# Where the operands of TensorE's products begin within a 64-byte line

## The chip, the cores and the metric

The kernel runs on one core of a Trainium2 chip. The metric is the device time of one execution in microseconds (us). Each comparison is between runs on the same chip.

## What is computed

One layer of a hybrid mixer over 1024 latent tokens and 256 context tokens, with a model width of 1024. The heads of both branches are 8, of width 128.

```python
h  = rms_norm(x) * (1 + scale) + shift            # the same for the context, with its own modulation
cols = h @ w_in                                    # q, k, v, z of branch A; q, k, v, z of branch B; two gates
# branch A: short convolution and silu on q, k, v; chunked gated delta rule in both directions
s_next = s * exp(gl) + kd.T @ (u - w @ s)
o_a    = qd @ s + qk @ v_new
# branch B: differential attention, two softmaxes a head, latents read context and latents
attn = softmax(q0 @ k0.T) - lam * softmax(q1 @ k1.T)
o_b  = attn @ v
# both branches: norm, silu gate, projection; then the merge
merged = g_a * (y_a @ w_oa) + g_b * (y_b @ w_ob)
out    = x + gate * (merged @ w_out)
```

All of it is float32. The large products are done in three parts with rounded operands (float32r): every factor is split into a high part, which is the rounded value, and a low part, the rest, and high x high, high x low and low x high are added up in PSUM.

## The kernel before

Everything is tiled to 128 partitions. A product on TensorE has a loaded operand (128 columns of weights, one weight load for each product) and a moving operand (256, 288 or 512 columns that stream past it). In the code `mm(out, lhsT, rhs)` at L55 loads `lhsT` and moves `rhs`; nearly all products go through its line L56, and turns (transposes on TensorE) through L63.

The stages in order of time:
- `front` (to about 105 us): loads, the normed tokens `hs` in high and low parts (`hgroup`), the modulation, and the first projection.
- `conv_start`, `conv_weights`, `conv_flow` (to about 400 us): projections of branch A's q, k, v. There the weights `wh`, `wl` are loaded and the tokens `hs` move, 512 or 256 columns at a time. Two parts of the kind "t" (the first two pairs of branch B's values) turn this round: `hs` is loaded and `wh`, `wl` move, 288 columns (with the columns for the decay gates) or 256.
- `part_weights`, `part_flow` (about 390 to 745 us): branch B's keys, further values and queries, ten parts, all in the turned-round form: `hs` loaded, 256 columns of `wh`, `wl` moving. Branch A's scan preparation (`gdn_prep`: `gram`, substitution on VectorE) runs between.
- `weights`, `fill_flow` (to about 1300 us): 32 units for the gates, 512 columns of `hs` moving, beside branch A's scan in float32 (`chain`, `out`).
- attention (about 1300 to 1755 us): `scores` (tile `s`: `qh`, `ql` loaded, `kk` moving), softmax on ScalarE, VectorE and GpSimd, `turns` (tile `t`: `S` loaded, the identity in `ct` moving), `high` and `low` (the turned weights in parts `ah`, `al`, L1636 and L1641), `att_out` (tile `v`: `vh`, `vl` loaded, 256 columns of `ah`, `al` moving), and branch A's merge `merge_` (tile `ma`, `y` moving).
- `b_main` (about 1766 to 1853 us): branch B's merge (tile `mb`): `wh`, `wl` of the pool `ws2` loaded, 512 columns of `yh`, `yl` of the pool `yq` moving.
- `o_main` (to the end): the output projection by seven half-size products (tiles `x`, `z`): `ah`, `al` loaded, `bh`, `bl` moving, from the pool `lp` for the even ones, `rp` and `bp` for the odd ones.

The order of every engine's instructions is written out by a planner inside the kernel: generators yield steps with an estimated cost, and `flow` or `turn_flow` picks the next one. It plans with costs alone, and not with addresses.

Addresses come from pools that lie in two stacks in each partition, one growing from the left, one from the right. A pool rounds each tile up to 32 bytes. A pool's tiles with the same tag share a place. Float32 words have 4 bytes, so 8 words are 32 bytes and 16 words one line of 64 bytes. In the kernel before, all operands of rounded products begin at a multiple of 64 bytes.

Of the kernel before, what the change touches and what calls it, by code (L numbers as in the profile page):

```python
# [8 lines left out]
F32 = mybir.dt.float32  # L9
F32R = mybir.dt.float32r  # L10
# [7 lines left out]
P = 128  # L18
D = 1024
KT = D // P  # L20
L = 1024
LC = 256
LT = L + LC
# [6 lines left out]
W = 256  # L30
# [13 lines left out]
class Block:  # L44
# [150 lines left out]
    def setup(self):  # L195
        nc, a = self.nc, self.a
        cp = self.cp = self.pool("const")
        self.dp = self.pool("spill", space=DRAM)
        ct = cp.tile([P, 3, P], F32, name="ct")
        nc.sync.dma_start(ct, a["consts"].rearrange("(a p) n -> p a n", p=P))  # L200
        self.ident, self.up, self.lo = (ct[:, i, :] for i in range(3))
        self.one = self.lo[:, 0:1]
        self.mhalf = cp.tile([P, 1], F32, name="mhalf")
        nc.gpsimd.memset(self.mhalf, -0.5)
        self.da = self.dp.tile([H, 2 * NT, 4, 32, 32], F32, name="da")
        self.db = self.dp.tile([H, 2 * NT, 4, 32, 32], F32, name="db")
        self.ya = self.dp.tile([2, H, P, L], F32, name="ya")
        self.yb = self.dp.tile([H, P, L], F32, name="yb")
        self.gkq = self.dp.tile([H, P, LT + L], F32, name="gkq")
        self.gkk = self.dp.tile([H, LT, P], F32, name="gkk")  # L210
        self.gv = self.dp.tile([H, LT, P], F32, name="gv")
        self.sza = self.dp.tile([H, P, L], F32, name="sza")
        self.szb = self.dp.tile([H, P, L], F32, name="szb")
        self.qd = self.dp.tile([2, H, P, L], F32, name="qd")
        self.kd = self.dp.tile([2, H, P, LT], F32, name="kd")
        self.vd = self.dp.tile([2, LT, H * P], F32, name="vd")
        self.gt = self.dp.tile([2 * KT, P, L], F32, name="gt")
        self.ma = self.dp.tile([KT, P, L], F32, name="ma")
        self.xq = self.dp.tile([H, P, 2, NT // 2, 2, 2, P], F32, name="xq")
        self.tbd = self.dp.tile([2, P, 1024], F32, name="tbd")  # L220
        self.gcd = self.dp.tile([2, H, LT], F32, name="gcd")
        self.gad = self.dp.tile([1, D], F32, name="gad")
        self.rbd = self.dp.tile([H, L], F32, name="rbd")
        for n in ("gkq", "gkk", "gv", "sza", "szb", "qd", "kd", "vd", "gt", "gcd", "ya", "yb"):
            self.dbg[n] = getattr(self, n).name


    @staticmethod
    def later(t, us):

        return t[0], t[1] + us

    def bank(self, name):

# [3 lines left out]
    def front(self, st, early, kv0):  # L238

        nc, a, cp, V = self.nc, self.a, self.cp, self.nc.vector  # L240
# [67 lines left out]
        def weights():  # L308
            for i, n in ((0, W), (1, W + 32)):
                yield lambda: (f"w{i}", 1) in T  # L310
                hl, ends = [self.wab[1 - i].tile([P, KT, n], F32R, tag=t, name=t) for t in ("wh", "wl")], []
                for s in range(2):
                    k = slice(s * KT // 2, (s + 1) * KT // 2)
                    for o, rw, us in ((0, raws[s], 0.256), (W, grw[:, k], 0.032))[:1 + i]:
                        c = slice(o, o + rw.shape[2])
                        t1 = yield ACT, 0.1 + 3.6 * us, [T[f"w{i}", s], T.get(("mm", 3))], lambda: nc.scalar.copy(hl[0][:, k, c], rw)
                        t2 = yield DV2, 4.7 * us, [t1], lambda: V.tensor_tensor(
                            hl[1][:, k, c], rw, hl[0][:, k, c].bitcast(F32), ALU.subtract)
                        ends += [t1, t2]
                    self.raw_t[s] = t2  # L320
                    if i == 0:
                        T["w", s] = [t1, t2]
                T["hl"] = T.get("hl", hl)
                if i:
                    self.parts_[1] = *hl, ends
# [122 lines left out]
    def conv_start(self, cols, right, late):  # L448

        self.copyq, self.tapq, self.siluq, self.normq, self.evq = [], [], [], ([], []), []  # L450
        self.copied, self.out_t, self.cdone, self.sq_t = {}, {}, set(), [None, None]
        self.row_t, self.sides, self.ringed = None, 0, 0
        self.ctiles = sum(2 for kind, _ in cols if kind in range(3))
        pools, last = self.wab, len(cols) - 1
        for q, b in ((self.copyq, 0), (self.tapq, 1), (self.siluq, 2), (self.normq[0], 2.5), (self.normq[1], 2.5), (self.evq, 0)):
            self.stream(self.forever(q), b)
        for g, b in ((self.gates(), 0.5), (self.lam_setup(), 0.6), (self.qk_tables(), 4), (self.gate_row(), 4)):
            self.stream(self.side(g), b)
        self.stream(self.conv_weights([c for _, c in cols], pools), 3)
        self.stream(self.conv_flow(cols), 9)  # L460
        done = lambda: len(self.cdone) >= self.ctiles and self.sides == 4 and not self.ringed
        self.stream(self.first(done, right, late), 6)
        self.turn_flow(lambda: last in self.parts_ and self.parts_done == last and self.head and not self.evq)
        self.ahead = self.parts_.pop(last)
        self.wab = pools if last % 2 else pools[::-1]
        self.streams = []
# [18 lines left out]
            x = next(g) if callable(x) else g.send((yield x))  # L485
        self.head = g, x

    def conv_weights(self, cols, pools):
        raw = lambda s: (self.wr.tile([P, KT // 2, W], F32, tag="wr", name="wr"), self.raw_t[s])
        for i, c0 in enumerate(cols):  # L490
            if i > 1:
                yield lambda: self.parts_done >= i - 1
                yield from self.weight(raw, *(pools[(i + 1) % 2].tile([P, KT, W], F32R, tag=n, name=n) for n in ("wh", "wl")),
                                       c0, W, [self.part_t.get(i - 2)], self.parts_, i, (DV2, DV2))

    def conv_flow(self, cols):
# [401 lines left out]
    def part_weights(self, parts):  # L898
        raw = lambda s: (self.wr.tile([P, KT // 2, W], F32, tag="wr", name="wr"), self.raw_t[s])
        for i, p in enumerate(parts):  # L900
            if i:
                yield lambda: self.parts_done >= i - 1
                yield from self.weight(raw, *(self.wab[i % 2].tile([P, KT, W], F32R, tag=n, name=n) for n in ("wh", "wl")),
                                       self.part_cols(*p), W, [self.part_t.get(i - 2)], self.parts_, i, (POOL, DV2))

    def fill_flow(self, todo):
# [178 lines left out]
    def gdn_prep(self, h):  # L1085
# [6 lines left out]

        def keys():
            S = lambda nm, shape: self.gh[0].tile(shape, F32, tag=nm, name=nm)
            kq, qk = S("kq", [P, LT + L + 8])[:, :LT + L], S("qk", [P, 2, 2, 2, P])
            kT, qT = kq[:, :LT], kq[:, LT:]
            tk = yield DMA, 3.3, self.kT_t, lambda: nc.sync.dma_start(kq, self.gkq[h])
            tk = tq = self.later(tk, 1.5)
            return kT, qT, qk, tk, tq
# [5 lines left out]
        for d in range(2):  # L1105
            for c in range(NT):
                t = yield ACT, 0.293, [self.later(ld, 2.0)], lambda: nc.scalar.activation(
                    X[:, d, c], X[:, d, c], AF.Abs, bias=self.gcc[:, c, d * H + h:d * H + h + 1], scale=-1.0)
            te[d] = yield ACT, 1.18, [t], lambda: nc.scalar.activation(X[:, d], X[:, d], AF.Exp, scale=-1.0), AF.Exp
        yield lambda: self.gram == h  # L1110
        kT, qT, qk, tk, tq = mine or (yield from keys())

        tX, tQ = [[], []], []
        for c0 in range(0, NT, 2):
            yield self.psum()
            b = self.banks.pop(0)
            pt = PT("gram")
            for j in range(2):
                c = c0 + j
                kc = kT[:, c * P:(c + 1) * P]  # L1120
                t = yield PE, 0.2235, [tk, b], lambda: self.mm(pt[:, j * 256:j * 256 + P], kc, kc)
                if c < NL:
                    t = yield PE, 0.2235, [tk, tq, b], lambda: self.mm(pt[:, j * 256 + P:j * 256 + 256], kc, qT[:, c * P:(c + 1) * P])
# [503 lines left out]
    def high(self, y, b, k, pt, t, bank):  # L1627

        nb, q = min(4, NT - 4 * k), slice(b * P, b * P + P)
        if b == 0:  # L1630
            yield lambda: self.open_ and self.vdone[k] >= y["i"]
            for a in ("ah", "al"):
                y[a, k] = self.a1.tile([P, nb, W], F32R, tag=f"{a}{k}", name=a)
            y["old", k], y["in", k] = self.vfree[k], []
        pv = pt[:, :nb * P].rearrange("p (j f) -> p j f", f=P)
        e = yield ACT, 0.48 if nb == 4 else 0.27, [t, y["old", k]], lambda: self.nc.scalar.copy(y["ah", k][:, :, q], pv)  # L1636
        self.lows.append((2 * y["i"] + 1, self.low(y, k, pv, q, e, bank)))
# [198 lines left out]
    def closing(self, zr, st, side):  # L1836
# [6 lines left out]
        self.a0s.close()  # L1843
        self.bp = self.spool(zr, "bp", side="right")
        for n in "hl":
            self.bp.tile([P, 4, 512], F32R, tag=f"b{n}", name="b" + n)
        sy = zr.enter_context(ExitStack())
        self.yq, self.stage = self.spool(sy, "yq", side="right"), 1
        yield lambda: H - 1 in self.yk and not self.groups and not self.mouts and self.wdone >= 16
# [361 lines left out]
```

## Time and profile before

| | |
|---|---|
| median of 3 runs | 1937.08 us (1934.67 to 1939.23) |
| profiled execution | 1935.46 us |
| its span, first to last instruction | 1933.3 us |
| mean granted clock of TensorE | 1.000 |
| busy: PE, PEld, DVE, ACT, POOL | 1896.7, 1675.3, 1453.0, 1062.6, 678.8 us |

PE is TensorE's products, PEld its weight loads, which overlap them, DVE is VectorE, ACT ScalarE, POOL GpSimd, SP the engine that issues the DMAs. A row of a group gives line, engine, operation, what is written <- what is read (moving operand first), shapes, count, then busy us and mean ns of one, then the idle time before them and what ended it. The mean of a product is its time in flight; the next one begins inside it.

### The profile page before, as it was taken

The page shows a single profiled execution, that of the slowest core. Times are in us where ns is not written, and L with a number is a line of the kernel's source. Part 1 is how long each engine was busy: PE and PEld are TensorE (multiplying, and loading weights), DVE is VectorE, ACT ScalarE, POOL GpSimd, SP SyncE. Part 2 cuts the span into 40 slices and gives each one's busy share as a digit, 9 for nine tenths or more (in the row PEclk, how much of TensorE's full clock was granted, in tenths as well). Part 3 has the DMA queues.
Part 4 walks back from the last instruction along what each step waited for, and adds up shares of the span by engine and source line. Part 5 has one row for each costly group of instructions (what it writes and reads, how often), then busy time and mean ns, then how long its engine had stood idle before and what let it go on. Part 6 is the DMA issues. An engine that isn't in the chain of part 4 may idle for free.

```text
span 1933.3 us, 37454 instructions
## 1 busy us (share of the span) xinstructions
PE 1896.7 (98%) x13807; PEld 1675.3 (87%) x13807; DVE 1453.0 (75%) x3613; ACT 1062.6 (55%) x2189; POOL 678.8 (35%) x610
## 2 busy tenths in 40 slices
PE   6999999999999999999999999999999999999999
PEld 4878888899999998888888888888997888888887
DVE  4687998957887887867865865338996979995677
ACT  4543444426233563677576645439885868884222
POOL 3200000005441342343333332336766667672203
PEclk9999999999999999999999999999999999999999
DMA  9144535575545567667785565666336474226542
GB/s 335 58 137 96 138 95 138 123 190 179 165 142 183 183 191 228 216 204 232 213 292 175 195 199 150 212 231 224 132 124 210 158 238 151 93 88 213 186 157 87
DMA packets 383038, 336.39 MB, mean 174 GB/s; under 512 B 142609, under 2 KB 323443, under 8 KB 381831
## 3 DMA queue, kind: packets, MB, share of 16 engines
q1 hardware_dynamic: 382855, 333.99, 55.0%
q8 instruction: 109, 1.79, 0.4%
q14 instruction: 74, 0.61, 0.1%
HBM read 222.14 MB, written 111.79 MB: 173 GB/s over the span
## 4 chain that ended last, share of the span: by engine, by line
PE 84%; DVE 6%; DMA 4%; ACT 3%; issue 2%; SPq 1%; POOL 1%; DVEq 0%; ACTq 0%; POOLq 0%
PE mm L56 43%; PE s L56 7%; PE v L56 5%; PE chain L56 5%; PE mb L56 5%; PE ma L56 4%; PE x L56 3%; PE t L63 3%; PE out L56 3%; PE gram L56 1%; DVE S L1567 1%; DVE ac L595 1%; PE pz L56 1%; PE tr L63 1%; SPq L265 1%
## 5 line engine op out<-in xcount | busy, mean ns | idle before, releaser
L56 PE MATMUL mm<-hs,wh 128*128 128x512 f32 (+1 forms) x2048 | 648.7, 390 | 1.5 <-DVE hs L408 1.4
L56 PEld LDWEIGHTS mm<-hs,wh 128*128 128x128 f32 x2048 | 371.3, 189 | 58.7 <-DVE hs L408 2.0
L56 PE MATMUL mm<-hs,wl 128*128 128x512 f32 (+1 forms) x1024 | 397.8, 388 | 1.0 <-POOL wl L886 1.0
L56 PE MATMUL mm<-wh,hs 128*128 128x256 f32 (+1 forms) x1792 | 332.7, 286 | 0.2 <-ACT sq L978 0.2
L56 PEld LDWEIGHTS mm<-wh,hs 128*128 128x128 f32 x1792 | 281.0, 191 | 0.7 <-ACT sq L978 0.4
L1567 DVE TENSOR_SCALAR_CACHE_REDUCE S<-s,rsq 128x512 f32<-128x512 f32 (+1 forms) x384 | 239.8, 655 | 26.9 <-DMA vl<-vd 12.0
L56 PE MATMUL mm<-wl,hs 128*128 128x256 f32 (+1 forms) x896 | 256.0, 286 | 0.0
L1604 POOL TENSOR_TENSOR S<-S 128x1280 f32<-128x1280 f32 x64 | 188.9, 2955 | 92.2 <-ACT S L1597 90.9
L56 PEld LDWEIGHTS mm<-hs,wl 128*128 128x128 f32 x1024 | 194.0, 189 | 29.8 <-POOL wl L886 1.4
L1580 ACT ACTIVATE S<-S,mn 128x1280 f32<-128x1280 f32 x128 | 175.2, 1372 | 51.3 <-DVE mn L1579 50.9
L56 PEld LDWEIGHTS mm<-wl,hs 128*128 128x128 f32 x896 | 171.4, 191 | 0.1
L595 DVE SCALAR_TENSOR_TENSOR ac<-xc,convT,ac 128x1284 f32<-128x1284 f32 (+1 forms) x96 | 138.8, 1448 | 11.2 <-ACT ac L593 10.6
L56 PE MATMUL s<-kk,qh 128*128 128x512 f32 (+1 forms) x384 | 142.7, 372 | 1.9 <-DVE S L1567 1.7
L56 PE MATMUL s<-kk,ql 128*128 128x512 f32 (+1 forms) x384 | 132.9, 358 | 0.0
L1641 DVE TENSOR_TENSOR al<-t,ah 128x512 fp32r<-128x512 f32 (+1 forms) x192 | 107.0, 595 | 7.6 <-ACT ah L1636 6.3
L580 POOL MEMSET xc<- 128x2 f32 (+1 forms) x64 | 3.6, 100 | 298.5 <-ACT sq L629 113.1
L1160 DVE TENSOR_TENSOR ts<-ts,tmp 80x31 f32<-80x31 f32 (+15 forms) x248 | 94.1, 380 | 6.0
L1323 ACT ACTIVATE vd<-chain,edk 128x128 f32<-128x128 f32 x144 | 52.2, 370 | 77.8 <-PE chain L56 71.9
L56 PE MATMUL ma<-y,wh 128*128 128x512 f32 x256 | 93.0, 410 | 1.7 <-DVE g L1814 1.7
L1158 DVE TENSOR_TENSOR tmp<-ab,ts 80x31 f32<-80x31 f32 (+15 forms) x248 | 89.2, 360 | 6.6 <-DMA ab<-da 1.3
L1636 ACT CAST ah<-t 128x512 fp32r<-128x512 f32 (+1 forms) x192 | 87.9, 521 | 9.0 <-PE t L63 8.3
L56 PE MATMUL v<-al,vh 128*128 128x256 f32 x320 | 90.9, 284 | 0.7 <-DVE al L1641 0.6
(296 smaller groups left out, 4315.7 us busy)
## 6 DMA issues: line engine op xcount, KB each, us to landing
wr<-in_w_in_dram SPq DMA_DIRECT2D x48, 512.0 KB, 5.7
hx<-in_w_in_dram SPq DMA_DIRECT2D x64, 256.0 KB, 4.3
x<-xq SPq DMA_DIRECT2D x64, 256.0 KB, 5.1
X<-gcd SPq DMA_DIRECT2D x8, 1280.0 KB, 7.1
kd<-col SPq DMA_DIRECT2D x40, 256.0 KB, 2.2
xq<-X SPq DMA_DIRECT2D x16, 640.0 KB, 8.9
kk<-kd SPq DMA_DIRECT2D x16, 640.0 KB, 6.4
kq<-gkq SPq DMA_DIRECT2D x8, 1152.0 KB
```

Source lines behind the costliest of these rows:

```text
L56: self.nc.tensor.matmul(out, lhsT, rhs, start=start, stop=stop)
L63: self.nc.tensor.transpose(out, src, self.ident[:src.shape[0], :src.shape[0]])
L265: return DMA, us, list(deps), lambda: nc.sync.dma_start(dst, src)
L595: t = yield DV2, 1.21e-3 * wd, [t], lambda: nc.vector.scalar_tensor_tensor(ac[:, :wd], xc[:, j:j + wd], self.convw(j, x["ct"]), ac[:, :wd] ...
L1158: t = yield DV2, n * w / 960.0 + 0.08, [t if j else self.later(t, 2.5), t1], lambda: V.tensor_tensor(tv, ab[:, j + 1:, j:j + 1].to_broadca ...
L1160: t = yield DV2, n * w / 960.0 + 0.08, [t, t1], lambda: V.tensor_tensor(ts[:, j + 1:, :w], ts[:, j + 1:, :w], tv, ALU.subtract)
L1323: td = yield ACT, 0.251, [t], lambda: nc.scalar.activation(vd, pc[:, 1], AF.Copy, scale=self.edk[:, c, g:g + 1])
L1567: e = yield DVE, 0.675 if m == 512 else 0.408, [e, self.sfree[c].get(n - 4 + c)], lambda: self.nc.vector.tensor_scalar(x["S"][c][:, o:o + ...
L1580: x["x"].append((yield ACT, 1.36, [e], lambda: nc.scalar.activation(S, S, AF.Exp, bias=x["mn"][:, c:c + 1], scale=-1.0, accum_out=w["l0"][ ...
L1604: e = yield POOL, 2.9, [e], lambda: self.nc.gpsimd.tensor_tensor(S0, S0, S1, ALU.add)
L1636: e = yield ACT, 0.48 if nb == 4 else 0.27, [t, y["old", k]], lambda: self.nc.scalar.copy(y["ah", k][:, :, q], pv)
L1641: t = yield DVE, 0.603 if k < 2 else 0.322, [e, y["old", k]], lambda: self.nc.vector.tensor_tensor(y["al", k][:, :, q], pv, y["ah", k][:, ...
```

## The change

It moves start addresses in SBUF. A helper, `at`, makes a tile that is 16 words longer than needed (one line) and returns the wanted part of it from word `off` on. Tiles `wh`, `wl` of the token-major parts and `ah`, `al` of attention start 8 words into their place; those `wh`, `wl` that are loaded start at word 0 of theirs. `mhalf` takes 9 words where it took 1, which shifts what follows it and the left stack by 32 bytes. `kq` loses its 8 spare words, which shifts the rest of the right stack by 32 bytes. The tile that reserves `bh` gets 8 more words.

```diff
-        self.mhalf = cp.tile([P, 1], F32, name="mhalf")
+        self.mhalf = cp.tile([P, 9], F32, name="mhalf")[:, 0:1]
...
+    @staticmethod
+    def at(pool, k, n, tag, off, name):
+
+        return pool.tile([P, k * n + 16], F32R, tag=tag, name=name)[:, off:off + k * n].rearrange("p (k n) -> p k n", k=k)
...
-                hl, ends = [self.wab[1 - i].tile([P, KT, n], F32R, tag=t, name=t) for t in ("wh", "wl")], []
+                hl, ends = [self.at(self.wab[1 - i], KT, n, t, 8 * i, t) for t in ("wh", "wl")], []
...
-        self.stream(self.conv_weights([c for _, c in cols], pools), 3)
+        self.stream(self.conv_weights([c for _, c in cols], pools, [i for i, (k, _) in enumerate(cols) if k not in range(3)]), 3)
...
-    def conv_weights(self, cols, pools):
+    def conv_weights(self, cols, pools, moving):
...
-                yield from self.weight(raw, *(pools[(i + 1) % 2].tile([P, KT, W], F32R, tag=n, name=n) for n in ("wh", "wl")),
+                yield from self.weight(raw, *(self.at(pools[(i + 1) % 2], KT, W, n, 8 if i in moving else 0, n) for n in ("wh", "wl")),
...
-                yield from self.weight(raw, *(self.wab[i % 2].tile([P, KT, W], F32R, tag=n, name=n) for n in ("wh", "wl")),
+                yield from self.weight(raw, *(self.at(self.wab[i % 2], KT, W, n, 8, n) for n in ("wh", "wl")),
...
-            kq, qk = S("kq", [P, LT + L + 8])[:, :LT + L], S("qk", [P, 2, 2, 2, P])
+            kq, qk = S("kq", [P, LT + L]), S("qk", [P, 2, 2, 2, P])
...
-                y[a, k] = self.a1.tile([P, nb, W], F32R, tag=f"{a}{k}", name=a)
+                y[a, k] = self.at(self.a1, nb, W, f"{a}{k}", 8, a)
...
-            self.bp.tile([P, 4, 512], F32R, tag=f"b{n}", name="b" + n)
+            self.bp.tile([P, 4 * 512 + 8 * (n == "h")], F32R, tag=f"b{n}", name="b" + n)
```

## The prediction

> **What bounds the kernel now.** I read the engines' busy times first, then the chain that ended last, then the groups of TensorE's instructions with their shapes kept apart, then the order of time inside them.
>
> ```profile
> span 1933.3 us, 37454 instructions
> ...
> PE 1896.7 (98%) x13807; PEld 1675.3 (87%) x13807; DVE 1453.0 (75%) x3613; ACT 1062.6 (55%) x2189; POOL 678.8 (35%) x610
> ...
> PE 84%; DVE 6%; DMA 4%; ACT 3%; issue 2%; SPq 1%; POOL 1%; DVEq 0%; ACTq 0%; POOLq 0%
> ```
>
> TensorE is busy 98% of the span and holds 84% of the chain that ended last. What shortens its products shortens the kernel, as long as nothing behind it becomes the limit. The products that the change speaks of are in these groups (matmuls, count, busy us, mean ns of one):
>
> ```profile
> L56 PE MATMUL mm<-wh,hs 128*128 128x256 f32 x1632 | 300.5, 285 | 0.2 <-ACT sq L978 0.2
> L56 PE MATMUL mm<-wl,hs 128*128 128x256 f32 x816 | 232.3, 285 | 0.0
> L56 PE MATMUL v<-al,vh 128*128 128x256 f32 x320 | 90.9, 284 | 0.7 <-DVE al L1641 0.6
> ...
> L56 PE MATMUL mb<-yh,wl 128*128 128x512 f32 x128 | 49.8, 389 | 0.0
> ...
> L56 PE MATMUL mm<-wh,hs 128*128 128x288 f32 x160 | 32.3, 296 | 0.0
> L56 PE MATMUL mm<-wl,hs 128*128 128x288 f32 x80 | 23.6, 295 | 0.0
> ```
>
> The mean of one (285 ns) is how long a product is in flight, not what it costs, since the next one starts inside it. The cost is the step from start to start. Three rows of the chain in order of time give it where nothing else is mixed in (start, us, pieces):
>
> ```profile
> 566.79 28.66 PE mm L56 x239
> 1766.26 87.04 PE mb L56 x384
> 1885.94 43.53 PE x L56 x192
> ```
>
> 28.66 / 239 = 119.9 ns for a product of 256 columns, 87.04 / 384 = 226.7 ns for one of 512. The difference, 106.8 ns for 256 more columns, is 0.417 ns a column. So 256 columns stream in 106.7 ns, and each product carries about 13.2 ns that its columns do not explain, the same in both sizes. Those 13 ns are all that the placing of operands can act on.
>
> **The change part by part.** No instruction is added or taken away; only byte addresses move, so every DMA keeps its count, its size and its queue. Where an operand lies is worked out from the tile sizes, which the pools round up to 32 bytes. Before, every operand of the rounded (fp32r) products begins at byte 0 of a 64-byte line.
> - The longer `mhalf` takes 64 bytes for 32 and pushes all that follows it and all left pools (`hs`, `wh`/`wl`, `ws2`, `yp2`, `a1`, `lp`) to byte 32. The shorter `kq` does this to the pools on the right below it (`a0` with `vh`, `vl`, `qh`, `kk`, `S`; `g1`, `g4`). That costs nothing by itself: it is the same difference between the operands. The products of 512 columns (convolution, gates, scores, `ma`) have both operands at 32 where both were at 0.
> - `at` with an offset of 8 words brings the moving `wh`/`wl` of the token-major parts and the moving `ah`/`al` back to byte 0, while their loaded partners `hs`, `vh`, `vl` stay at 32. These are 1632 + 816 = 2448 products of 256 columns, 160 + 80 = 240 of 288, and 3 x 320 = 960 `v`. It takes 64 bytes more a tile; the gaps between the left and right pools are larger than that.
> - `bh` lengthened by 8 words puts `yq` back to byte 0, so `yh`/`yl` move from 0 and `ws2` is loaded from 32: 3 x 128 = 384 products `mb`. By the way `bl` in `bp` comes to 32 against `ah` at 0, in three of the seven last products (48 matmuls): bounded below at no change and above by 48 x 3.3 ns = 0.2 us (the 3.3 ns are derived with the last rival).
> - The turns `t<-ct,S` go from (0, 0) to moving 0, loaded 32. The front's turns had that placing already; compare the rows:
>
> ```profile
> 50.13 0.60 PE L63 MATMUL pt<-ct,x 128*128 128x128 f32 x4
> ...
> 1372.57 1.25 PE L63 MATMUL t<-ct,S 128*128 128x128 f32 x10
> ```
> ```profile
> L63 PE MATMUL t<-ct,S 128*128 128x128 f32 x640 | 86.1, 273 | 0.8 <-DVE al L1641 0.8
> ```
>
> One turn is 0.273 us in flight, so the four of the front step at (0.60 - 0.273) / 3 = 0.109 and the ten of attention at (1.25 - 0.273) / 9 = 0.109 us. Loaded at 32 or at 0, a turn costs the same: no term.
>
> So the sum is 4032 products times an unknown gain, which no row of this trace shows, since none of its rounded products is placed (0, 32). Bounds by the nearest rows, the steps of an fp32 product whose weight load is as long:
>
> ```profile
> L56 PEld LDWEIGHTS mm<-wh,hs 128*128 128x128 f32 x1792 | 281.0, 191 | 0.7 <-ACT sq L978 0.4
> ...
> L56 PEld LDWEIGHTS gram<-kq 128*128 128x128 f32 x288 | 37.8, 192 | 1.5 <-ACT t L1199 0.6
> ```
> ```profile
> 501.99 1.06 PE L56 MATMUL gram<-kq 128*128 128x128 f32 x8
> ```
> ```profile
> L56 PE MATMUL gram<-kq 128*128 128x128 f32 x288 | 42.3, 276 | 0.2 <-ACT t L1199 0.2
> ```
>
> Eight passes of `gram` (0.276 us each in flight) step at (1.06 - 0.276) / 7 = 0.112 us with loads of 192 ns against 191. So a load of 128 columns can follow the last one after 112 ns, and the most that a product of 256 columns can gain by this row is 120 - 112 = 8 ns: 32 us for 4032. From above, the products could lose up to 3.3 ns (13 us) by reading across one line more, which is worked out with the last rival. What lies between is seen in the trace itself, where short runs of `v` start:
>
> ```profile
> 1433.92 0.27 PE L56 MATMUL v<-al,vh 128*128 128x256 f32 x1
> 1434.03 0.28 PE L56 MATMUL v<-ah,vl 128*128 128x256 f32 x1
> 1434.15 0.28 PE L56 MATMUL v<-ah,vh 128*128 128x256 f32 x1
> 1434.26 0.39 PE L56 MATMUL s<-kk,qh 128*128 128x512 f32 x1
> ```
>
> Single steps of 0.11 us between two `v`, and from a `v` to the next product, occur in the same placing (1433.92 to 1434.03, 1434.15 to 1434.26), beside the usual 0.12. I read the 13 ns as the loading of the next weights getting in the way of the moving reads: the loads run beside the products (PEld is busy 87% of the span, PE 98%), and at (0, 0) both would walk the same half lines. If the half-line shift parts the two, the step falls to about 113 ns, just above the 112 of the load itself. I take 7 ns a product, near the lower end because both the shortest steps and `gram` lie there:
> - token-major parts: 2448 x 7 = 17.1 us
> - the part of 288 columns: 240 x 7 = 1.7 us
> - attention's `v`: 960 x 7 = 6.7 us
> - merge of branch B: 384 x 7 = 2.7 us
>
> That is 28.2 us. [...]
>
> What covers it must hold when TensorE is quicker. Three windows of all engines (us of the window, PE, PEld, DVE, ACT, POOL), and after each kind one of the tile `mm` or `v` alone:
>
> ```profile
> 500.00:550.00 50.00, 49.90 (x421) 49.65 (x420) 47.31 (x113) 16.53 (x35) 26.29 (x17) 1.00 0.43 134
> ...
> 700.00:745.00 45.00, 45.00 (x348) 43.35 (x347) 42.82 (x113) 25.97 (x63) 13.87 (x9) 1.00 0.61 198
> ```
> ```profile
> 500.00:550.00 50.00, 45.41 (x361) 43.62 (x360) 0.00 (x0) 9.20 (x24) 1.00 0.43 134
> ```
> ```profile
> 1350.00:1400.00 50.00, 50.00 (x340) 45.24 (x338) 46.21 (x160) 41.88 (x72) 35.77 (x19) 1.00 0.41 137
> ```
> ```profile
> 1350.00:1400.00 50.00, 19.44 (x135) 18.32 (x135) 2.41 (x7) 1.45 (x4) 1.00 0.41 137
> ```
>
> Of the 421 matmuls in 500 to 550, 361 are `mm` of 256 columns and would save 2.5 us, which leaves 47.5 us for 47.3 us of VectorE: there it becomes the limit, and 700 to 745 with 42.8 of 45 us is no better. I take back 2 us for these two windows. In attention at most 135 `v` save 0.9 us of 50, and 49.1 stand against 46.2 us of VectorE, so PE still ends last; I take back 1 us. Net 25.2 us: the profiled execution's 1935.5 (span 1933.3 and 2.2 around it) becomes 1910.3. The median of the runs is 1937.1, 1.6 above, so 1912.
>
> **The rivals.**
> - *Half of it goes.* The load takes as long as the product streams (about 112 against 107 ns), so a shift may only trade some meetings for others. Half the gain, 3.5 ns x 4032 = 14 us, less 1.5 of VectorE's: 1925. For it: steps of 0.11 and 0.12 alternate in one placing in the rows of `v`. Against it: the long runs hold 119.9 and 226.7 ns to a tenth, so what stops a product is regular.
> - *Nothing happens: 1937.* The 13 ns are a hand-over from one set of weights to the next, whatever the address. For it: the same 13 in 256 and 512 columns, and turns that do not care where they load from. Against it: `gram` hands over too, at 112 ns for a stream of 256 columns' time or less. [...]
> - *Slower.* What begins at byte 32 and is a multiple of 64 bytes long touches one line more. If that costs the time of half a line of moving data, 8 columns x 0.417 = 3.3 ns, every product now placed (32, 32) pays it. Their counts:
>
> ```profile
> L56 PE MATMUL mm<-hs,wh 128*128 128x512 f32 x1792 | 602.2, 405 | 1.5 <-DVE hs L408 1.4
> L56 PE MATMUL mm<-hs,wl 128*128 128x512 f32 x896 | 361.5, 403 | 1.0 <-POOL wl L886 1.0
> ...
> L56 PE MATMUL ma<-y,wh 128*128 128x512 f32 x256 | 93.0, 410 | 1.7 <-DVE g L1814 1.7
> ```
> ```profile
> L56 PE MATMUL s<-kk,qh 128*128 128x512 f32 (+1 forms) x384 | 142.7, 372 | 1.9 <-DVE S L1567 1.7
> ```
>
>   1792 + 896 of the convolution and the gates, 2 x 384 of scores, 256 + 128 of `ma`: 3840 x 3.3 = 12.8 us. With no gain, 1950. It decides once the gain is below 12.8 / 4032 = 3.2 ns a product. [...]
>
> **How the numbers follow.** Full gain 0.38, half 0.24, nothing 0.23, slower 0.15. A measurement of this kernel tells about 0.2% (4 us) from no change: faster 0.62, same 0.23, slower 0.15. The prediction is the likeliest case, 1912. The lower end is the 8 ns bound in full, 1937 - 32 = 1905; the upper end must take in the case of nothing with its spread, 1940. If it is faster, 1905 to 1930.
>
> **What would show it.** The long piece of `mm` near 567 us at 113 ns a product and `mb` at 220 ns would show the gain, with VectorE above 95% in 500 to 550. Steps of 119.9 and 226.7 again would show the hand-over. `x` above 226.7, or `ma` and the fill's products of 512 columns at 230 and more, would show straddling. I am wrong if the gain depends on the size of the product, or if the reuse of shifted memory adds a wait at a pool's opening that is now hidden.

## The result, and the profile after

The change makes the kernel slower: 1945.62 us in the median (1943.00 to 1947.24) against 1935.12 us of the kernel before on the same chip (1934.67 to 1939.23), a ratio of 1.0048 with a 95% interval of 1.0036 to 1.0059. The forecast was 1912 us. The profiled execution took 1947.24 us (span 1945.1); that of the kernel before 1935.46 (1933.3). The page of the changed kernel (span, busy us of the engines, the shares of the chain that ended last):

```profile
span 1945.1 us, 37454 instructions
...
PE 1905.3 (98%) x13807; PEld 1671.4 (86%) x13807; DVE 1451.2 (75%) x3613; ACT 1063.5 (55%) x2189; POOL 679.3 (35%) x610
...
PE 83%; DVE 7%; DMA 4%; ACT 3%; issue 2%; POOL 1%; SPq 1%; DVEq 0%; ACTq 0%; POOLq 0%
```

The instructions are the same and TensorE is as full as before (98% of the span), but it is busy 8.6 us longer. The chain in order of time (start, us, pieces) tells which products grew. Of the kernel before, two pieces that the prediction did not show: a run of the convolution (178 products of 512 columns and 48 of 256) and the first of the last products.

```profile
275.41 46.27 PE mm L56 x226
...
1853.30 21.76 PE x L56 x96
```

The same chain of the changed kernel:

```profile
277.58 47.06 PE mm L56 x226
...
569.33 28.19 PE mm L56 x239
...
1774.67 89.59 PE mb L56 x384
1864.26 21.99 PE x L56 x96
1897.19 44.07 PE x L56 x192
```

The long run of the parts, 28.66 us before, is 28.19: 118.0 ns for 119.9, a gain of 2 ns where 7 were forecast. `mb` went from 226.7 to 233.3 ns (89.59 / 384), and should have fallen to 220. The convolution's run grew by 0.79 us although nothing was meant to change there, and the last products by 0.23 and 0.54 us.

For the whole kernel I put each of the 13807 records beside the addresses that the program gives its operands, and took the step from one product's start to the next. "Settled" are steps with a product of the same size two before, one before and one behind, and no wait in between:

| products | settled | ns before | ns after | difference, us |
|---|---|---|---|---|
| parts, 256 columns | 2295 of 2448 | 119.8 | 118.2 | -3.8 |
| parts, 288 columns | 234 of 240 | 133.3 | 132.3 | -0.2 |
| `v`, 256 columns | 697 of 960 | 119.1 | 118.2 | -0.6 |
| convolution, 256 columns | 334 of 384 | 119.9 | 117.7 | -0.7 |
| convolution and gates, 512 columns | 1784 of 2688 | 227.9 | 231.6 | +6.8 |
| `mb`, 512 columns | 384 of 384 | 226.7 | 233.3 | +2.6 |
| `x`, 512 columns | 285 of 288 | 226.6 | 229.4 | +0.8 |

With the small rows left out here, settled steps give +5.3 us. The other steps (at the ends of runs, with waits, and between kinds) give some 6 us more, which is less sure, since it sets one execution against one; no address is shown to be the cause of those. Two waits among them are longer, by the view of TensorE's waits over the whole span (before first, then after; us in total, times, longest):

```profile
PE tr L63 <- DVE fin L1000: 1.0, 1, 1.0
...
PE chain L56 <- DMA sk<-gkq: 0.7, 1, 0.7
```
```profile
PE chain L56 <- DMA sk<-gkq: 2.9, 2, 1.8
...
PE tr L63 <- DVE fin L1005: 2.6, 2, 1.6
```

So the parts gained 3.8 us in their settled steps and gave 2.0 back in the others. What the settled steps lost, they lost in the products of 512 columns.

### The profile page after: what moved, and what is told of

Same layout as the page of the kernel before. It is cut to its first block, busy times and chain, and to the rows that moved or that the text cites. A ratio compares the mean times of both kernels' runs of the same rounds, so it can differ in the third digit from the quotient of the medians.

```text
span 1945.1 us, 37454 instructions
## 1 busy us (share of the span) xinstructions
PE 1905.3 (98%) x13807; PEld 1671.4 (86%) x13807; DVE 1451.2 (75%) x3613; ACT 1063.5 (55%) x2189; POOL 679.3 (35%) x610
## 4 chain that ended last, share of the span: by engine, by line
PE 83%; DVE 7%; DMA 4%; ACT 3%; issue 2%; POOL 1%; SPq 1%; DVEq 0%; ACTq 0%; POOLq 0%
PE mm L56 42%; PE s L56 7%; PE v L56 5%; PE chain L56 5%; PE mb L56 5%; PE ma L56 4%; PE x L56 3%; PE t L63 3%; PE out L56 3%; DVE S L1572 1%; PE gram L56 1%; DMA sk<-gkq 1%; DVE ac L600 1%; PE tr L63 1%; PE pz L56 1%
## 5 line engine op out<-in xcount | busy, mean ns | idle before, releaser
L56 PE MATMUL mm<-wh,hs 128*128 128x256 f32 (+1 forms) x1792 | 328.8, 283 | 0.3 <-ACT sq L983 0.3
L600 DVE SCALAR_TENSOR_TENSOR ac<-xc,convT,ac 128x1284 f32<-128x1284 f32 (+1 forms) x96 | 138.8, 1448 | 12.4 <-ACT ac L598 11.8
```

What stands on the lines that cost most here:

```text
L56: self.nc.tensor.matmul(out, lhsT, rhs, start=start, stop=stop)
L600: t = yield DV2, 1.21e-3 * wd, [t], lambda: nc.vector.scalar_tensor_tensor(ac[:, :wd], xc[:, j:j + wd], self.convw(j, x["ct"]), ac[:, :wd] ...
```

## The experiments

Times are medians; ratios are to the kernel before on the same chip as each run, with 95% intervals. The runs are spread over several chips. Steps in ns, and what they add up to, come from the one profiled execution of each kernel.

**Is it the byte 32, by touching one line more (straddling)?** The kernel before with the longer `mhalf` and the shorter `kq` alone: everything begins at byte 32, moving and loaded.

```diff
-        self.mhalf = cp.tile([P, 1], F32, name="mhalf")
+        self.mhalf = cp.tile([P, 9], F32, name="mhalf")[:, 0:1]
...
-            kq, qk = S("kq", [P, LT + L + 8])[:, :LT + L], S("qk", [P, 2, 2, 2, P])
+            kq, qk = S("kq", [P, LT + L]), S("qk", [P, 2, 2, 2, P])
```

> The kernel before with only the two shifts (`mhalf`, `kq`): every rounded product is placed (32, 32), nothing is staggered. Theory A: nothing changes, 227 and 120 ns a product, ratio 0.999 to 1.001. Theory B, byte 32 costs by itself: 230 ns and more for the products of 512 columns, 8 to 13 us more, ratio 1.004 to 1.007.

Measured: 1937.30 us, ratio 1.0001 (0.9992 to 1.0010). Its chain has the steps of the kernel before, to the last digit:

```profile
275.89 46.27 PE mm L56 x226
...
567.30 28.66 PE mm L56 x239
...
1770.03 87.04 PE mb L56 x384
```

Byte 32 by itself costs nothing that these runs can tell. The rival's mechanism for a loss, 12.8 us, is refuted.

**Is it the spare words?** `at` makes each tile 64 bytes longer, so `wl` begins 64 bytes later against `wh` and `hs` than it did. The kernel before with these spare words alone, everything at byte 0 of a line:

```diff
+    def at(pool, k, n, tag, off, name):
+        return pool.tile([P, k * n + 16], F32R, tag=tag, name=name)[:, :k * n].rearrange("p (k n) -> p k n", k=k)
```

> The kernel before with only the 16 spare words of `at`, at offset 0: every rounded operand still begins at byte 0 of a 64-byte line, but `wl` and `al` 64 bytes further than `wh` and `ah` within 128. Theory A: the products of 512 columns of convolution and gates go to 230 to 236 ns, 8 to 9 us more; those of 256 columns may gain 1 to 3 ns; merge stays at 227; ratio 1.002 to 1.005. Theory B: nothing changes, ratio 0.999 to 1.001, 227 and 120 ns.

Measured: 1941.93 us, ratio 1.0028 (1.0019 to 1.0038), which is 5.4 us slower. The run of the convolution takes what it takes in the changed kernel, `mb` does not move, and the parts gain a little:

```profile
275.78 47.06 PE mm L56 x226
...
568.61 28.31 PE mm L56 x239
...
1770.31 87.05 PE mb L56 x384
```

About half of the loss is a by-product: 64 bytes that nobody meant to place anything with.

**What is the period?** I took it for 128 bytes and laid the spare words so that `wh` and `wl` agree modulo 128 again, in the changed kernel:

```diff
-        return pool.tile([P, k * n + 16], ...)[:, off:off + k * n]
+        spare, off = (24, 24 if off else 0) if tag == "wh" else (8, 0 if off else 8) if tag == "wl" else (32, 24)
+        return pool.tile([P, k * n + spare], ...)[:, off:off + k * n]
```

> The changed kernel with one thing undone: the spare words in `at` are laid so that `wl` begins at the same byte of a 128-byte stretch as `wh` (in the changed kernel it is 64 bytes further), and `al` as `ah`. All else is as changed: convolution and gates (32, 32), token-major parts and `v` (0, 32), merge of branch B (0, 32). Theory A, the stagger of 64 bytes between `wh` and `wl` slows the products of 512 columns: convolution and fill return from 230 to 236 ns to 227 ns a product, 8 to 9 us less than the changed kernel, a ratio to before of 0.999 to 1.003. Theory B, byte 32 itself costs, whatever the partner: the steps stay at 230 to 236 ns and the ratio at 1.0048. Theory C, the products are not it, waits are (sk, fin): ratio within 0.001 of 1.0048 with the steps changed or not.

Measured: 1944.91 us, ratio 1.0043 (1.0030 to 1.0056), and

```profile
276.65 47.13 PE mm L56 x226
```

The loss stayed: with 128 bytes between them the steps are as long as with 64. My theory failed in this form. Two kernels that run nothing but products in groups (18 equal ones, or 30 in a pattern), and leave the whole computation out, then measured the step against the two addresses.

> Only products and their loads, on one tile of moving and one of loaded data; nothing of the layer is computed and the output is a copy of an input. Runs of 18 products of 256 and of 512 columns, moving from byte 0, 16, 32, 64 or 96 and loaded from byte 0, 8, ... 120 of a 128-byte stretch, then runs of 30 that alternate as the kernel does. Theory A: with one constant placing 512 columns take 227 ns and 256 take 120 when the two differ by a multiple of 64 bytes, others differ by some ns (mb at (0, 32) took 233, v about 118); runs that alternate by 64 bytes take 230 to 236 ns in 512 columns. Theory B: what depends is only the byte of the moving operand: 227 at 0 and 64, 230 or more at 32 and 96, the same for all loaded bytes.

The first map found that the difference, loaded minus moving, sets the step as long as the moving operand begins at a multiple of 32 bytes: with a difference of 0 it is about 120 ns for 256 columns and 226.7 for 512, with the moving operand at 32, 64 or 96 and, but for the first group of 512 columns (228.4), at 0; at (0, 32) 118.4 and 233.3; and 113.3 ns at single places, (0, 64) among them. With the moving operand at byte 16 the pattern is another one: (16, 16) takes 118.3 and 231.1 ns, and 226.8 for 512 columns stands at (16, 48). So the difference is not the whole rule; every rounded operand of the kernels here, though, begins at a multiple of 32. The second map went up to 504 bytes.

> This kernel leaves out the whole computation and runs groups of products of one kind back to back, each group with the moving operand at one byte offset and the loaded operand at another, all offsets counted from a multiple of 512 bytes: the moving one at 0 and the loaded one at 0, 8, ... 504, with 256 and with 512 columns; then the moving one at 64, 128 and 192; then patterns that shift every third product by 32, 64, 128 or 256 bytes. Theory A, the step is set by the difference of the two addresses modulo 256 bytes: 512 columns take 226.7 ns at a difference of 0 and of 256, and 229 to 234 at 128 and at every other multiple of 32; 256 columns take 120 ns at 0 and 256, near 113 at one or two offsets (64 among them) and 115 to 119 elsewhere; the row of 0 to 248 repeats from 256 to 504; a pattern shifted by 256 bytes costs nothing, one shifted by 128 costs 2 to 7 ns in the mean. Rival B, the period is 128 bytes: 128 and 384 read as 0 does, 226.7 and 120. Rival C, it is 512 or none at all and what counts is that the placing changes from product to product: 256 differs from 0 by 2 ns and more, and a pattern shifted by 256 costs as much as one shifted by 64.

Pieces of its chain (start, us, 18 products each), 256 columns, moving at 0, loaded at 0, 32, 64, 128, 192, 256, 320:

```profile
21.00 2.15 PE saa L39 x18
...
29.54 2.13 PE sae L39 x18
...
38.04 2.05 PE sai L39 x18
...
54.99 2.13 PE saq L39 x18
...
72.03 2.12 PE say L39 x18
...
88.98 2.16 PE sbg L39 x18
...
106.12 2.05 PE sbo L39 x18
```

and 512 columns, loaded at 32, 64, 128, 192, 256, 376:

```profile
173.70 4.20 PE lae L39 x18
...
190.50 4.20 PE lai L39 x18
...
223.96 4.19 PE laq L39 x18
...
257.43 4.12 PE lay L39 x18
...
290.71 4.10 PE lbg L39 x18
...
353.48 4.09 PE lbv L39 x18
```

Settled steps, without a group's first five:

| difference, bytes | 0 (256) | 32 | 64 | 88 | 120 | 128 | 168 | 192 |
|---|---|---|---|---|---|---|---|---|
| 256 columns, ns | 120.0 (120.1) | 118.4 | 113.3 | 113.3 | 119.2 | 118.4 | 113.3 | 117.8 |
| 512 columns, ns | 228.8 (226.7) | 233.3 | 233.3 | 233.3 | 226.7 | 232.8 | 233.3 | 228.9 |

All 32 places from 0 to 248 repeat from 256 to 504 within 1 ns, but for 0 with 512 columns (the first group after a change of size, 228.8, not yet settled), and 24 and 48 with 256 columns (122.3 and 117.8 against 118.8 and 123.3). So the period is 256 bytes, and a few differences have more than one step: 96 with 256 columns takes 117.3 ns with the moving operand at 0 and 120.0 with it at 64, 128 or 192. A pattern in which every third product is shifted by 256 bytes costs nothing (226.7), one shifted by 64 takes 231.2 in the mean, near the 231.6 of the convolution and the gates in the changed kernel, where `wl`, every third weight, lies 64 bytes off. A difference of 0 is close to the worst for 256 columns and the best for 512; 32 is worth 1.6 ns to the one and costs the other 6.6.

**The merge alone.** The changed kernel without the 8 words in `bp`, so that `yh`, `yl` and `ws2` differ by 0 again:

```diff
-            self.bp.tile([P, 4 * 512 + 8 * (n == "h")], F32R, tag=f"b{n}", name="b" + n)
+            self.bp.tile([P, 4, 512], F32R, tag=f"b{n}", name="b" + n)
```

> The changed kernel without the 8 words more in the last buffers of the merge, so that the merge of branch B has both operands at byte 32. Theory A (the difference of the addresses sets the step, and with 512 columns a difference of 0 is the best there is): the products mb go from 233 back to 227 ns, 384 x 6.5 = 2.5 us, and the first of the last x products back to 227, 0.6 us; the time against the kernel before goes from 1.0048 to about 1.0033, 1942.5 us. Rival (what I predicted: byte 32 against byte 0 helps a product whatever its columns, and mb lost for another reason such as its late start): mb stays at 233 or more, the time stays at 1.0048 or grows.

Measured: 1940.65 us, ratio 1.0024 (1.0015 to 1.0033). `mb` and the last products are back:

```profile
1771.12 87.09 PE mb L56 x384
1858.21 21.76 PE x L56 x96
1890.85 43.53 PE x L56 x192
```

That is 3.3 us in these stages (2.50 + 0.23 + 0.54); the ratios differ by 4.6 us, which agrees within their intervals.

**The change without its by-products, and a better difference.** Both halves of a set of weights lie in one tile, so that they shift together; `v` is shifted by words in front of `a1`. Three kernels: differences of 0 as a control; 32 bytes in the parts and in `v`; 64 bytes there. Everything of 512 columns keeps its old difference.

```diff
+    def pair(self, pool, n, moving):
+        first = pool is self.wa
+        off = (48 if first else 0) if moving else (0 if first else 16)      # 64 bytes; 56 and 8 words give 32
+        t = pool.tile([P, 2 * KT * n + (48 if first else 16)], F32R, tag="whl", name="whl")
+        return [t[:, off + i * KT * n:off + (i + 1) * KT * n].rearrange("p (k n) -> p k n", k=KT) for i in (0, 1)]
...
+        self.a1.tile([P, 48], F32, tag="pad", name="pad")
```

> The kernel before with the upper and the lower half of a set of weights in one tile and all differences of addresses as before (0 modulo 256 bytes); a control for the two that follow. Every theory: 256 columns 119.8 ns, 512 columns 226.7, ratio 0.999 to 1.001, unless the common tile adds a wait.

> The control with what the change says and none of its side effects: in the token-major parts and in v the loaded operand lies 32 bytes behind the moving one modulo 256 for both halves of the weights, and every product of 512 columns (the merge mb too) keeps a difference of 0. Theory A (difference modulo 256): 256 columns take 118.4 ns, as in the map, 3408 products x 1.4 ns = 4.8 us less, 512 columns stay at 226.7; ratio 0.997 to 0.999 against before. Theory of the prediction (7 ns a product, spoilt in the changed kernel only by the uneven spacing of its tiles): 113 ns, 24 us less, some 5 of them lost to waits, ratio 0.988 to 0.991.

> The same with 64 bytes for 32. Theory A: 256 columns lock at 113.3 ns as in the map, 3408 x 6.5 = 22 us less before waits; VectorE and the turns that wait for it give back 3 to 8 us; 1917 to 1922 us, ratio 0.990 to 0.993. Rival (the lock of the map needs a stream with nothing between, and waits of the kernel break it): 116 to 118 ns, ratio 0.996 to 0.998. Rival (VectorE is the limit behind TensorE): 113.3 ns inside the runs, but longer idle time, ratio above 0.996.

> The kernel before with 192 bytes in front of the tiles of attention's moving operand, so that v alone has its loaded operand 64 bytes behind the moving one; nothing else moves. Theory A: v goes from 119.8 to 113.3 ns where several follow each other, 960 x 6.5 = 6.2 us at most, less what the short groups of v lose at their ends: 1930 to 1932, ratio 0.997 to 0.998. Rival (in attention TensorE has slack behind VectorE): v is quicker and the time stays, ratio 0.9995 to 1.0005.

| kernel | us | ratio | parts, settled ns | `v`, settled ns |
|---|---|---|---|---|
| control, 0 | 1936.46 | 0.9999 (0.9990 to 1.0008) | 119.9 | 119.1 |
| 32 bytes | 1934.29 | 0.9990 (0.9981 to 0.9999) | 118.3 | 118.2 |
| 64 bytes | 1930.61 | 0.9969 (0.9956 to 0.9981) | 114.4 | 116.0 |
| 64 bytes in `v` alone | 1934.34 | 0.9991 (0.9982 to 0.9999) | 119.8 | 115.9 |

With 32 bytes, then with 64, the chain shows the same 239 and 226 products:

```profile
275.82 46.27 PE mm L56 x226
...
565.99 28.28 PE mm L56 x239
```
```profile
274.14 46.27 PE mm L56 x226
...
561.70 27.10 PE mm L56 x239
```

So what the change says is worth 1.6 ns a product and about 2 us; at 64 bytes this run stands at 113.4 ns (27.10 / 239), the 113 that I had forecast for 32. That version is the fastest of all, 5.0 us below the kernel before and, on another chip, 15 below the changed one. But even there I expected 13 to 18 us and got 5.9 against the control. With 64 bytes in `v` alone I expected a ratio of 0.997 to 0.998, and got 0.9991.

The first reason is that a difference of 64 bytes has two steps. Two runs of the parts at 64 bytes, a few us apart:

```profile
545.40 5.80 PE mm L56 x51
...
551.75 5.19 PE mm L56 x44
```

Without the first five products the one settles at 113.3 ns, the other at 117.8. Of the 44 runs of 8 or more steps of the parts, 29 settle at 113.3 to 113.5 ns and 15 at 117.6 to 117.8; of the 38 such runs of `v`, 23 near 113.3 and 15 near 117.8. That is how 114.4 and 116.0 come about. In the second map, groups at (0, 64) that follow seven products of 512 columns settled at 113.3 ns six times and at 117.8 twice. What decides between the two is open.

The second is a wait. Steps of the parts, control against 64 bytes: 2287 settled ones save 12.4 us; 29 steps from a product to a turn grow from 189 to 331 ns and give back 4.1; 10 steps inside runs that have a wait give back 1.0. (These two profiled executions differ by 9.4 us, more than the medians do. Three of the eight runs at 64 bytes, those of 1932.7 to 1934.2 us, had a mean granted clock of 0.998; the other five, 0.999 to 1.000, took 1928.0 to 1931.7.) The waits of TensorE from 400 to 745 us, of the control, then of the 64 bytes:

```profile
PE tr L63 <- DVE fin L1008: 0.8, 1, 0.8
...
PE tr L63 <- POOL fin L1016: 0.2, 1, 0.2
```
```profile
PE tr L63 <- DVE fin L1008: 2.8, 2, 2.6
PE tr L63 <- POOL fin L1016: 1.1, 4, 0.5
```

The turns `tr` wait for `fin`, the normed and rotated columns of an earlier tile, which VectorE and GpSimd finish.

**Is it VectorE's pace?** Control and 64 bytes again, with less work there (the last step of the rotation is left out):

```diff
-                te += [(yield DV2, 0.35, [t1, t2], lambda: V.tensor_tensor(o[hf], o[hf], m[hf],
-                                                                          (ALU.subtract, ALU.add)[hf]))]
+                te += [t1, t2]
```

> The control with the tiles in pairs and differences of 0, with less work on VectorE in the token-major parts: the last step of the rotation (one of three tensor_tensor for each half) is left out. Every theory: TensorE's products take 119.8 ns as before and end last, ratio 0.996 to 1.001.

> The same with the loaded operand 64 bytes behind the moving one in the parts and in v; read against the run with differences of 0 and the same step left out, since both issue the same instructions in the same order. If the waits for VectorE took what the quicker products saved (full VectorE: 6.8 of 13 us were left in the parts), the difference grows to 12 to 16 us, ratio 0.992 to 0.994 between the two. Rival (the saving is lost in other places, at the starts of the short runs or in waits that have nothing to do with VectorE): the difference stays at 5 to 9 us.

Measured: 1942.05 (1.0030, 1.0021 to 1.0040, more than any theory allowed; the planner lays another order) and 1934.17 us (0.9988, 0.9980 to 0.9997), 7.9 us apart in one and the same order. In the window from 500 to 550 us (PE, PEld, DVE, ACT, POOL), the 64 bytes with the full work, then with less:

```profile
500.00:550.00 50.00, 49.50 (x426) 48.76 (x426) 47.09 (x116) 14.35 (x32) 25.44 (x17) 1.00 0.41 127
```
```profile
500.00:550.00 50.00, 48.94 (x417) 47.78 (x416) 42.67 (x100) 17.24 (x36) 27.10 (x18) 1.00 0.38 118
```

VectorE fell from 47.1 to 42.7 us, and still 35 steps to a turn grew from 181 to 262 ns, 2.8 us. The pair falls inside the rival's 5 to 9 us: with VectorE less busy the turns still gave back 2.8 us of the 4.1, so its share of busy time accounts for a third of that at most.

**Is it the planned order?** The planner reckons 119.5 ns a product; the same pair with 114.3:

```diff
-                            t = yield PE, 0.1195, [free[self.nb], tw], lambda: self.mm(
+                            t = yield PE, 0.1143, [free[self.nb], tw], lambda: self.mm(
```

> The control with the tiles in pairs and differences of 0; the planner that lays down the order of the instructions is told 114.3 ns for a product of the token-major parts in place of 119.5. The products still take 119.8 ns, so the turns come a little late for what waits on them. Every theory: ratio 0.998 to 1.003.

> The loaded operand 64 bytes behind the moving one in the parts and in v, with the planner told 114.3 ns. Theory W (part of the saving was turned into waits because the order, planned for 119.5 ns, puts the turns of the parts' results too early for the quicker products): the 29 steps from a product to a turn go from 331 ns back to about 200, 4 us, and the time to 1924 to 1927 us, 10 to 12 us below the run with the same plan and differences of 0. Rival (VectorE's own pace holds the turns back wherever they stand in the order): the waits stay or move to another place; 1929 to 1933 us, 5 to 7 us below the run with differences of 0.

Measured: 1963.56 (1.0140, 1.0126 to 1.0154) and 1955.35 us (1.0094, 1.0077 to 1.0110), 8.2 us apart, between the two expectations. Those for the level were missed: the other order costs 27 us (1963.56 against 1936.61 of the kernel before on that chip). Its runs also had a lower mean granted clock, 0.996 to 0.997 against 0.999 to 1.000, which in proportion would be some 6 of them, an estimate. In the pair the settled steps save 11.7 us, and 31 steps to a turn grow from 220 to 312 ns, 2.8 us. So the waits stay in an order planned for quick products too. Three orders, the same picture: some 12 us saved in the settled steps of the parts, 3 to 4 given back before the turns. The steps before a turn are shown to be the place; what sets the time of `fin` (the latency of its chain over the engines, or the planner's estimates for it) is open.

## Why the prediction was wrong

- **What the products cost.** That TensorE is the bound holds (98% of the span in both profiles, 84% and 83% of the chain). The step that failed is the next one: the 13.2 ns beyond the columns were "the same in both sizes", and I read that as one cost, which a shift lowers in both. That they came out the same was no evidence: 0.417 ns a column and 13.2 ns are worked out from those two steps, and two steps always give one slope and one remainder. They belong to the difference 0 alone. There a product of 256 columns, at 120.0 ns, lies near the long end (113.3 to 123.3), and one of 512, at 226.7, is at the short end (226.7 to 234.2). From there a shift helps the one at most places and can only harm the other. At the shortest steps, 113.3 and 226.7, twice the columns take twice the time, and no remainder is left. That the gain depends on the size of the product is what the prediction itself had named as a sign of being wrong.
- **The gain of 7 ns.** Measured 1.6 in the parts, 1.0 in the part of 288 columns and 0.9 in `v`. The bound of 112 ns from `gram` was not broken by any difference, and 113.3 exists, 32 bytes further on. The choice of 113 rested on single steps of 0.11 us of `v` at the ends of its short runs. The rows were right, but these steps do not last: `v` settles at 119.1 before the change.
- **`mb`.** Forecast -2.7 us, measured +2.6. The sign was wrong, for the reason of the first point.
- **"That costs nothing by itself: it is the same difference between the operands."** True for `mhalf` and `kq` (ratio 1.0001). But I compared addresses modulo 64 bytes and took the spare line of `at` for memory alone. It moves `wl` by 64 bytes, the period is 256, and 2688 products of 512 columns paid: 6.8 us in settled steps, and the whole kernel 5.4 us by the ratio when only this was done. The sum put it at nothing, and the range ended at 1940, though "slower" stood at 1950 with a chance of 0.15. Nor does any run show a unit of 64 bytes.
- **`bl`.** Bounded at 0 to 0.2 us; the stages of the last products took 0.8 us more. The bound came from the straddling price, which no run shows.
- **The turns `t`** were given no term: the 640 of attention changed by -0.06 us together. Right.
- **The cover.** I took 3 us back of 28. With steps of 114.4 ns the turns alone took 4.1 of 12.4 us in the parts. Even with the right difference the gain was some 6 us, not 25. The windows tell that VectorE is nearly full (from 500 to 550 us, 47.3 us before and 47.1 with 64 bytes); they do not tell how soon after `fin` is ready its turn stands in the order.
- **The rivals.** "Slower" had the right sign and nearly the size (1950), but by luck: the first experiment refutes its mechanism (ratio 1.0001 with everything at byte 32). "Nothing happens" took the 13 ns for a hand-over that costs the same whatever the address. The runs disagree: with nothing but the difference of two addresses changed, a product of 256 columns takes 113.3 to 123.3 ns in the second map.

## What to carry to other kernels

Before moving an operand, write down the difference of loaded and moving address modulo 256 bytes (the period in the second map) for every product that reads from the same tiles, and not only for those that you mean to change: a tile made longer by a few words shifts all that lie behind it. Keep operands that are used together in one tile, so that they move together. Take the sign of a placement from a run for each size of product (a difference of 32 bytes took 1.6 ns off 256 columns here and put 6.6 on 512); and when a step gets shorter, look at what the next turn or wait in the written order is waiting for: here the steps to a turn gave back 4.1 of the 12.4 us saved in the parts.

## What the runs showed of the hardware

With a weight load for each product of rounded operands, the step in the two maps depends on where the two operands lie to each other: 113.3 to 123.3 ns for 256 columns, 226.7 to 234.2 ns for 512, in uniform streams with the moving operand at a multiple of 32 bytes. It repeats after 256 bytes (second map, moving operand at 0, loaded operand from 0 to 504). With the moving operand at byte 16 the same differences gave other steps in the first map, up to 236.7 ns for 512 columns at (16, 32). One difference can have two steps: 64 bytes gave 113.3 or 117.8 ns for 256 columns, in the map and in the kernel, and a run of the kernel's parts held the one or the other after its first five products. A new group needs some products to settle: the first group of 512 columns in the second map took 228.8 ns, where the same difference, 256 bytes on, took 226.7. A pattern of three that varies the difference mostly gives a step in between (226.7 and 233.3 gave 231.2). 64 and 192 bytes mixed (two products and one) hold 113.3 ns too. What inside the chip meets at these addresses, the runs do not show.
